# A hybrid block on one core: one channel tile of the depthwise convolution on GpSimd, the mLSTM's row normalisation on ScalarE

## The chip, the cores and the metric

The kernel runs on one NeuronCore of a Trainium2 chip. The metric is the device time of one launch in microseconds (us). A profile of one execution goes with it; in it PE is TensorE, PEld its weight loads, DVE is VectorE, ACT is ScalarE, POOL is GpSimd and SP is SyncE, which here issues the DMAs. "L494" is line 494 of the kernel before.

## The reference, cut to what matters

Two layers (`l = 0, 1`) over a sequence of 512 tokens and a context of 256, width 1024. Each layer has a token mixer with three branches and a squared-ReLU MLP. All is float32.

```python
def conformer_conv(a, w_dw, b_dw, g, b, w_pw):
    val, gate = jnp.split(a, 2, axis=-1)
    h = val * jax.nn.sigmoid(gate)
    h = lax.conv_general_dilated(h, w_dw[:, None, :], (1,), ((15, 15),),      # 31 taps, each of
                                 feature_group_count=CONV_DIM) + b_dw          # 512 channels alone
    return jax.nn.silu(layer_norm(h, g, b)) @ w_pw

def mlstm_out(h, o_pre, g, w):                  # h: mLSTM forward + backward, 4 heads of 128
    mu = jnp.mean(h, -1, keepdims=True)
    var = jnp.mean(jnp.square(h - mu), -1, keepdims=True)
    h = ((h - mu) * lax.rsqrt(var + LN_EPS)).reshape(bsz, t, ML_DIM) * g
    return (jax.nn.sigmoid(o_pre) * h) @ w

def token_mixer(...):
    a, qkv, o_pre, g_if, cq, ckv, kr, gates = jnp.split(u @ w_in + b_in, IN_SPLITS, axis=-1)
    y_conv = conformer_conv(a, ...)
    y_ml = mlstm_out(mlstm_bidir(...), ...)     # chunks of 128 tokens, state carried from chunk to chunk
    o_x = mla_blockwise(...)                    # latent attention, 8 heads
    return gated_merge(gates, y_conv, y_ml, o_x @ w_mla_out, w_out, b_out)
```

In layer 0 sequence and context (768 columns) go through all of it; in layer 1 the convolution, the gates and the MLP see the 512 sequence columns alone.

## The kernel before, in words

**Layout.** Activations lie channel-major: 128 channels on the partitions, up to 768 tokens along the free axis. The layer's input `u` is eight such tiles. The convolution's 512 channels are four tiles, `hc[0]` to `hc[3]`, with an accumulator `ca[j]` each.

**Products.** Every large product is made of three passes over a high and a low part of both operands (`mm3`, L266 to L268). A weight tile comes by DMA (`wr`), ScalarE makes its high part `wh` (L261), and the low part `wl` is a subtraction `wr - wh` (L262). That subtraction is on VectorE, except for the weights of the 24 gate tiles and the four output-gate tiles, where `plan()` names GpSimd. Weights are fetched two ahead (`LOOK = 2`); raw, high and low part have three buffers each.

**The stage around the change**, in each layer, in the order of the program:

1. Four times value and gate of the convolution: two products, ScalarE's identity and tanh, and one VectorE instruction (L511) make `hc[j]`.
2. V, gates of the mLSTM and the key's rotary part (L526 to L548): 2 x 6 groups of 24 products, each evacuated from one of the two `pg` tiles of PSUM by VectorE (L541, L544, L548).
3. Cumulated gates, scans and exponentials on 36 rows (L551 to L615), then the K and Q products (L618 and L640).
4. The mLSTM: six chunks in each direction (`mstep`). When both directions of a row tile are there, `mnorm` normalises it: `bn_stats` and `bn_aggr` per head on VectorE, `EPS` added (L745), the power -0.5 on GpSimd (L746), and per head one VectorE instruction, subtract the mean and multiply by the power (L748).
5. The 24 gate products, each with a tanh and a store to DRAM. After the eleventh the convolution's layer norm is done (`ln_fm`, L784), which reads all four `ca`.

**The taps.** `conv_taps()` is a generator. For each of four channel tiles it issues one VectorE instruction for the middle tap with the bias (L488), and then for each of 30 other taps one fused multiply-add per segment (L494): `ca += hc[shifted] * w`. Layer 0 has two segments (512 and 256 columns, less the shift), layer 1 one. `some_taps(k)` draws k taps from the generator; calls stand between the steps of stages 1 to 5 (9 after each `hc[j]`, 2 in each group of stage 2, 4 and 5 after each K and Q product, 3 after each gate), and the rest is drawn before the layer norm. The modulation vectors for later (`mod_pieces`, L165) are drawn in the same way with `pull`.

**What sets the order.** Only the first products are put in order by hand. Elsewhere the program's order gives priorities and a planner lays each engine's instructions in one fixed queue; an instruction that waits holds all behind it on its engine. Tiles come from pools of fixed size: `slot()` takes one of the 35 buffers of the pool `gen`.

Of the kernel before, what the change touches and what calls it, by code (L numbers as in the profile page):

```python
# [44 lines left out]
def build(tc, I, out):  # L45
    nc = tc.nc
# [1 line left out]
    ctx = ExitStack()  # L48
    cp = ctx.enter_context(tc.tile_pool(name="const", bufs=1))
    wp = ctx.enter_context(tc.tile_pool(name="w", bufs=3))  # L50
    gp = ctx.enter_context(tc.tile_pool(name="gen", bufs=35))
    vp = ctx.enter_context(tc.tile_pool(name="v", bufs=12))
    mp = ctx.enter_context(tc.tile_pool(name="mw", bufs=8))
    sp = ctx.enter_context(tc.tile_pool(name="small", bufs=6))
# [398 lines left out]
    for l in range(L):  # L453
# [26 lines left out]
            return [(0, n, win(i, n)[:, :n])]  # L480

        def conv_taps():
            for j in range(4):
                acc = slot("ca")
                ca.append(acc)
                wd = lambda t: col(l, "w_dw", j * CK + t)
                h = hc[j]
                V.tensor_scalar(acc[:, :n], h[:, :n], wd(15), col(l, "b_dw", j), op0=OP.mult, op1=OP.add)  # L488
                for d in [x for i in range(1, 16) for x in (-i, i)]:
                    for s0, s1 in ((0, S), (S, n)):  # L490
                        if s1 <= s0:
                            continue
                        a, b = max(s0, s0 - d), min(s1, s1 - d)
                        V.scalar_tensor_tensor(acc[:, a:b], h[:, a + d:b + d], wd(15 + d), acc[:, a:b],  # L494
                                               op0=OP.mult, op1=OP.add)
                    yield

        taps = None

        def some_taps(k):  # L500
            for _ in range(k):
                next(taps, None)

        for j in range(4):
            val, tg = slot("val"), slot("tg")
            for c0, c1, ps in conv_in(MT_VAL + j):
                A.activation(val[:, c0:c1], ps, AF.Identity, bias=HB(MT_VAL + j), scale=0.5)
            for c0, c1, ps in conv_in(MT_GATE + j):
                A.activation(tg[:, c0:c1], ps, AF.Tanh, bias=HB(MT_GATE + j), scale=0.5)
            h = slot("hc")  # L510
            V.scalar_tensor_tensor(h[:, :n], tg[:, :n], 1.0, val[:, :n], op0=OP.add, op1=OP.mult)  # L511
            hc.append(h)
            if j == 0:
                taps = conv_taps()
            some_taps(9)


        vt = []
# [7 lines left out]
        for hf, w_n in ((0, VG0), (1, VG1)):  # L526
            ws = [wget("w_vg", l, hf * 2 + q) for q in range(2)]
            for tt in range(NT):
                ps = pg()
                t0 = tt * 128  # L530
                for k in range(8):
                    wh, wl = ws[k // 4]
                    a, b = (k % 4) * w_n, (k % 4 + 1) * w_n
                    uh, ul = u[k]
                    o = ps[:, :w_n]
                    PE.matmul(o, uh[:, t0:t0 + 128], wh[:, a:b], start=(k == 0), stop=False)  # L536
                    PE.matmul(o, uh[:, t0:t0 + 128], wl[:, a:b], start=False, stop=False)  # L537
                    mark[0] = PE.matmul(o, ul[:, t0:t0 + 128], wh[:, a:b], start=False, stop=(k == 7))  # L538
                some_taps(2)
                bo = hf * VG0  # L540
                V.tensor_tensor(vt[tt][:, 2 * hf:2 * hf + 2, 0:128], ps[:, 0:256].rearrange("p (h d) -> p h d", h=2),  # L541
                                bvg[:, bo:bo + 256].rearrange("p (h d) -> p h d", h=2), op=OP.add)
                if hf == 0:
                    V.tensor_tensor(gt[:, tt, :].rearrange("p (g j) -> p g j", g=4)[:, :, 0:4],  # L544
                                    ps[:, 256:272].rearrange("p (g j) -> p g j", g=4),
                                    bvg[:, 256:272].rearrange("p (g j) -> p g j", g=4), op=OP.add)
                else:
                    V.tensor_tensor(kr[:, tt, :], ps[:, 256:288], bvg[:, VG0 + 256:VG0 + 288], op=OP.add)  # L548
# [69 lines left out]
        for h in range(MH):  # L618
            ps = win(MT_K + h, T)
            t = slot("kT")  # L620
            A.activation(t, ps, AF.Identity, bias=kb[l][:, h:h + 1], scale=KSCALE)
            kT.append(t)
            some_taps(4)
        kinds = {}
        for name, src in (("g", g_), ("A", A_), ("W", W_), ("E", E_)):
            ps = pt()
# [13 lines left out]
        for h in range(MH):  # L640
# [1 line left out]
            t = slot("qT")  # L642
            A.activation(t[:, :n], ps[:, :n], AF.Identity, bias=B(MT_Q + h))
            qT.append(t)
            some_taps(5)


        cst_ = [cp.tile([128, 4, 129], F32, name=f"cs{l}{d}", tag=f"cs{d}") for d in range(2)]
# [88 lines left out]
        def mnorm(tt):  # L737
# [6 lines left out]
            rs = small(4, "mrs", 3)  # L744
            V.tensor_scalar(rs, mv.rearrange("p (h s) -> p h s", s=2)[:, :, 1], EPS, None, op0=OP.add)  # L745
            G.tensor_tensor(rs, rs, mhalf, op=OP.pow)  # L746
            for h in range(MH):
                V.tensor_scalar(hv[:, h, 0:128], hv[:, h, 0:128], mv[:, 2 * h:2 * h + 1], rs[:, h:h + 1],  # L748
                                op0=OP.subtract, op1=OP.mult)
            hnorm[tt] = hv  # L750

        for j in range(NT):
# [23 lines left out]
        for b in range(3):  # L776
            for mt in range(8):
                g = gate(b, mt)
                nc.sync.dma_start(z_dram[b, mt, :, :n], g[:, :n])
                some_taps(3)  # L780
                pull(2)
                if b * 8 + mt == 10:
                    some_taps(200)
                    ln_fm(ca, 4, groups, conv_emit)  # L784


# [507 lines left out]
```

## Time and profile before

| | |
|---|---|
| median of 3 runs | 2558.47 us (2554.23 to 2559.24) |
| the profiled execution's own time | 2557.35 us |
| its span in the profile | 2555.5 us |
| PE busy | 2470.4 us (97%) |
| DVE busy | 1580.6 us (62%) |
| ACT busy | 939.5 us (37%) |
| POOL busy | 298.7 us (12%) |
| taps (L494), both layers | 227.8 us in 360 instructions |
| normalisation on DVE (L748) | 19.4 us in 40 instructions |
| gate weights' low parts on POOL (L262) | 145.7 us in 56 instructions |
| granted PE clock | 0.993 |

Busy time is the time in which an engine has an instruction running; an engine that is blocked inside an instruction counts as busy. A line of a view by groups has line, engine, operation, output and inputs, shapes and count, then busy time, mean ns of one, and the engine's idle time just before them with what ended it. A timeline row has start, duration, engine, line, operation, operands and count. In a table by stretches each row has the length, and then the busy time of each engine with its number of instructions.

### The profile page before, as it was taken

What the parts mean: (1) busy time and instruction counts of PE and PEld (TensorE: products, weight loads), DVE (VectorE), ACT (ScalarE), POOL (GpSimd) and SP (SyncE); (2) the same over time, 40 slices, a digit from 0 to 9 for tenths busy, and PEclk for the clock granted to TensorE, in tenths of its full rate; (3) what the DMA queues carried; (4) which work ended last, traced back from release to release, by engine and by line L of the source; (5) the groups of instructions that cost most, each with busy time, mean ns of one, the idle gap of its engine ahead of it and who ended that gap; (6) DMA issues with size and microseconds to landing.
All of it is one profiled execution on the core that took longest, in us unless ns stands there. A gap on an engine that the chain in (4) does not pass through costs nothing.

```text
span 2555.5 us, 38339 instructions
## 1 busy us (share of the span) xinstructions
PE 2470.4 (97%) x15272; PEld 2163.8 (85%) x15272; DVE 1580.6 (62%) x2847; ACT 939.5 (37%) x1607; POOL 298.7 (12%) x235
## 2 busy tenths in 40 slices
PE   7899989999999999999999999999999999999997
PEld 5888878888888899888888888977888888888887
DVE  4999976363356777655554379996043567554456
ACT  3123323222457563222222253333324575432323
POOL 0002132203000021000000031023411001100002
PEclk9999999999999999999999999999999999999999
DMA  7122344466110654343342252233563106333333
GB/s 264 53 75 70 98 163 161 166 195 210 62 34 1 188 168 142 122 131 115 108 129 88 65 149 78 59 106 101 175 203 111 50 18 213 101 99 92 99 94 113
DMA packets 137235, 298.45 MB, mean 117 GB/s; under 512 B 13776, under 2 KB 55248, under 8 KB 137056
## 3 DMA queue, kind: packets, MB, share of 16 engines
q1 hardware_dynamic: 137056, 296.00, 36.9%
q8 instruction: 120, 1.97, 0.3%
q14 instruction: 59, 0.48, 0.1%
HBM read 265.49 MB, written 30.46 MB: 116 GB/s over the span
## 4 chain that ended last, share of the span: by engine, by line
PE 81%; DVE 9%; DMA 4%; ACT 2%; issue 2%; POOL 1%; SPq 0%; DVEq 0%; ACTq 0%; POOLq 0%
PE pg L266 21%; PE pg L267 21%; PE pg L268 21%; PE pt L1003 2%; PE pt L982 2%; PE pt L266 2%; PE pt L267 2%; PE pt L268 2%; DVE ca L494 2%; DMA wm<-w_mod 1%; DMA ml<-z_dram 1%; PE pg L536 1%; PE pg L538 1%; PE pg L537 1%; DVE st L315 1%
## 5 line engine op out<-in xcount | busy, mean ns | idle before, releaser
L261 ACT CAST wh<-wr 128x1024 fp32r<-128x1024 f32 (+1 forms) x328 | 345.6, 1055 | 1202.4 <-PE pg L267 825.5
L262 DVE TENSOR_TENSOR wl<-wr,wh 128x1024 fp32r<-128x1024 f32 (+2 forms) x272 | 338.6, 1246 | 410.1 <-ACT wh L261 406.3
L268 PE MATMUL pg<-uh,wl 128*128 128x512 f32 (+1 forms) x1280 | 456.3, 356 | 2.2 <-DVE wl L262 2.2
L266 PE MATMUL pg<-uh,wh 128*128 128x512 f32 (+1 forms) x1280 | 457.2, 357 | 1.2 <-ACT gt__17278 L760 1.2
L267 PE MATMUL pg<-ul,wh 128*128 128x512 f32 (+1 forms) x1280 | 455.5, 356 | 0.7 <-POOL ul L1171 0.6
L266 PE MATMUL pg<-hidh,wh 128*128 128x512 f32 (+1 forms) x832 | 285.4, 344 | 3.9 <-DVE mv L318 2.0
L267 PE MATMUL pg<-hidl,wh 128*128 128x512 f32 (+1 forms) x832 | 284.9, 342 | 0.0
L268 PE MATMUL pg<-hidh,wl 128*128 128x512 f32 (+1 forms) x832 | 284.2, 342 | 0.0
L266 PEld LDWEIGHTS pg<-uh,wh 128*128 128x128 f32 x1280 | 244.2, 191 | 35.4 <-issue 2.5
L268 PEld LDWEIGHTS pg<-uh,wl 128*128 128x128 f32 x1280 | 243.9, 191 | 34.4 <-DVE wl L262 2.7
L267 PEld LDWEIGHTS pg<-ul,wh 128*128 128x128 f32 x1280 | 244.1, 191 | 33.2 <-POOL ul L1171 1.0
L494 DVE SCALAR_TENSOR_TENSOR ca<-hc,cols,ca 128x511 f32<-128x511 f32 (+9 forms) x360 | 227.8, 673 | 2.4
L262 POOL TENSOR_TENSOR wl<-wr,wh 128x1024 fp32r<-128x1024 f32 x56 | 145.7, 2602 | 562.6 <-ACT wh L261 562.6
L267 PE MATMUL pg<-u2l,wh 128*128 128x512 f32 (+1 forms) x608 | 210.3, 347 | 0.3 <-POOL u2l L1082 0.2
L1139 DVE SCALAR_TENSOR_TENSOR acc<-pg,mod,acc 128x512 f32<-128x512 f32 (+1 forms) x168 | 106.0, 659 | 168.6 <-PE pg L268 168.6
L268 PE MATMUL pg<-u2h,wl 128*128 128x512 f32 (+1 forms) x608 | 210.1, 347 | 0.0
L266 PE MATMUL pg<-u2h,wh 128*128 128x512 f32 (+1 forms) x608 | 209.9, 347 | 0.0
L165 DVE SCALAR_TENSOR_TENSOR mda<-wm,sil,mda 128x512 f32<-128x512 f32 x224 | 176.2, 808 | 7.6 <-DMA wm<-w_mod 5.0
L266 PEld LDWEIGHTS pg<-hidh,wh 128*128 128x128 f32 x832 | 157.3, 190 | 25.3 <-issue 3.5
L321 POOL TENSOR_TENSOR rs<-rs,mhalf 128x1 f32<-128x1 f32 x30 | 24.4, 819 | 1298.5 <-DVE rs L320 1298.5
L267 PEld LDWEIGHTS pg<-hidl,wh 128*128 128x128 f32 x832 | 157.9, 190 | 18.7 <-DVE hidl L1129 1.6
L268 PEld LDWEIGHTS pg<-hidh,wl 128*128 128x128 f32 x832 | 157.7, 189 | 18.0
(359 smaller groups left out, 4754.1 us busy)
## 6 DMA issues: line engine op xcount, KB each, us to landing
wr<-w SPq DMA_DIRECT2D x140, 512.0 KB, 3.6
wr<-w_in_fm SPq DMA_DIRECT2D x104, 512.0 KB, 3.8
wm<-w_mod SPq DMA_DIRECT2D x192, 256.0 KB, 4.5
wr<-w_out SPq DMA_DIRECT2D x40, 512.0 KB, 3.9
ml<-z_dram SPq DMA_DIRECT2D x104, 128.0 KB, 2.8
ml<-z_dram SPq DMA_DIRECT2D x48, 256.0 KB, 4.4
z_dram<-ml SPq DMA_DIRECT2D x32, 256.0 KB, 4.5
dm<-m_dram SPq DMA_DIRECT2D x20, 256.0 KB, 4.4
```

What stands on the lines that cost most here:

```text
L165: ins = V.scalar_tensor_tensor(av[v], w, sil[:, k, v:v + 1], av[v], op0=OP.mult, op1=OP.add)
L261: A.copy(h[:, :n], r[:, :n])
L262: eng.tensor_sub(lo[:, :n], r[:, :n], h[:, :n])
L266: PE.matmul(ps, hs, xh, start=first, stop=False)
L267: PE.matmul(ps, hs, xl, start=False, stop=False)
L268: return PE.matmul(ps, ls, xh, start=False, stop=last)
L315: V.bn_stats(st[:, hf * 6:(hf + 1) * 6], ps)
L494: V.scalar_tensor_tensor(acc[:, a:b], h[:, a + d:b + d], wd(15 + d), acc[:, a:b], op0=OP.mult, op1=OP.add)
L536: PE.matmul(o, uh[:, t0:t0 + 128], wh[:, a:b], start=(k == 0), stop=False)
L982: PE.transpose(p2[:, y * 128:(y + 1) * 128], P[:, (k4 + y) * 128:(k4 + y + 1) * 128], ident)
L1003: PE.matmul(po[64 * i:64 * i + 64, :256], va[B_.k0 + k][:, h * 64:h * 64 + 64], B_.pts[i][k // 2][:, k % 2, :], start=(k == 0), stop=(k == ...
L1139: V.scalar_tensor_tensor(acc[mt][:, c0:c1], ps[:, c0:c1], mc[:, 40 + mt, v:v + 1], acc[mt][:, c0:c1], op0=OP.mult, op1=OP.add)
```

## The change

- `conv_taps()` now serves channel tiles 0 to 2. Tile 3 has a generator of its own, `pool_taps()`, on GpSimd. It has no fused multiply-add there: each tap is a multiplication of all columns into a scratch tile `pt` and one addition per segment onto `ca[3]`.
- `some_pool_taps(k)` draws from it: one in every third group of stage 2, 2 after each K product, Q product and gate, the rest ahead of the layer norm. VectorE's draws become 7, 1 or 2, 3, 3 and 2.
- The four accumulators are taken at the first tile instead of one by one.
- In `mnorm` a new VectorE instruction makes `-mean * power` for the four heads, and the four per-head instructions go to ScalarE as an activation with scale and bias.
- The pool `gen` has 38 buffers, and the program's scratch for DMA descriptors is set to 1024.

```diff
-    gp = ctx.enter_context(tc.tile_pool(name="gen", bufs=35))
+    gp = ctx.enter_context(tc.tile_pool(name="gen", bufs=38))
...
         def conv_taps():
-            for j in range(4):
-                acc = slot("ca")
-                ca.append(acc)
+            for j in range(3):
+                acc = ca[j]
...
-        taps = None
+        def pool_taps():
+
+            acc, h = ca[3], hc[3]
+            wd = lambda t: col(l, "w_dw", 3 * CK + t)
+            G.tensor_scalar(acc[:, :n], h[:, :n], wd(15), col(l, "b_dw", 3), op0=OP.mult, op1=OP.add)
+            for d in [x for i in range(1, 16) for x in (-i, i)]:
+                t = slot("pt")
+                G.tensor_scalar(t[:, :n], h[:, :n], wd(15 + d), None, op0=OP.mult)
+                for s0, s1 in ((0, S), (S, n)):
+                    if s1 <= s0:
+                        continue
+                    a, b = max(s0, s0 - d), min(s1, s1 - d)
+                    G.tensor_tensor(acc[:, a:b], acc[:, a:b], t[:, a + d:b + d], op=OP.add)
+                yield
+
+        taps = ptaps = None
...
+        def some_pool_taps(k):
+            for _ in range(k):
+                next(ptaps, None)
...
             if j == 0:
+                ca.extend(slot("ca") for _ in range(4))
                 taps = conv_taps()
-            some_taps(9)
+            some_taps(7)
+        ptaps = pool_taps()
...
-                some_taps(2)
+                some_taps(2 if hf else 1)
+                if tt % 3 == 2:
+                    some_pool_taps(1)
...
-            some_taps(4)
+            some_taps(3)
+            some_pool_taps(2)
...
-            some_taps(5)
+            some_taps(3)
+            some_pool_taps(2)
...
+            nm = small(4, "mnm", 3)
+            V.scalar_tensor_tensor(nm, mv.rearrange("p (h s) -> p h s", s=2)[:, :, 0], -1.0, rs,
+                                   op0=OP.mult, op1=OP.mult)
             for h in range(MH):
-                V.tensor_scalar(hv[:, h, 0:128], hv[:, h, 0:128], mv[:, 2 * h:2 * h + 1], rs[:, h:h + 1],
-                                op0=OP.subtract, op1=OP.mult)
+                A.activation(hv[:, h, 0:128], hv[:, h, 0:128], AF.Identity, bias=nm[:, h:h + 1], scale=rs[:, h:h + 1])
...
-                some_taps(3)
+                some_taps(2)
+                some_pool_taps(2)
                 pull(2)
                 if b * 8 + mt == 10:
                     some_taps(200)
+                    some_pool_taps(200)
                     ln_fm(ca, 4, groups, conv_emit)
...
-    nc = bacc.Bacc("TRN2", target_bir_lowering=False, num_devices=1)
+    nc = bacc.Bacc("TRN2", target_bir_lowering=False, num_devices=1, dynamic_dma_scratch_size=1024)
```

## The prediction

> **What bounds the kernel now.** I read the page first (span, engine totals, the digits over 40 slices), then the table of busy time by stretches, the waits of TensorE, and last the timelines of GpSimd and VectorE side by side.
>
> ```profile
> span 2555.5 us, 38339 instructions
> ...
> PE 2470.4 (97%) x15272; PEld 2163.8 (85%) x15272; DVE 1580.6 (62%) x2847; ACT 939.5 (37%) x1607; POOL 298.7 (12%) x235
> ...
> DVE  4999976363356777655554379996043567554456
> ```
>
> Over the whole span TensorE (PE) is the bound: 85.1 us of idle is all that any change to the other engines could win. But the digits show two places, one per layer, where VectorE (DVE) is full too. They are the convolution and the mLSTM, where this change acts. The table by stretches gives their size:
>
> ```profile
> core 0: us, PE busy (x) PEld busy (x) DVE busy (x) ACT busy (x) POOL busy (x), PEclk, DMA share, GB/s
> 100.00:150.00 50.00, 43.14 (x308) 42.20 (x307) 47.44 (x117) 8.94 (x11) 0.00 (x0) 0.93 0.17 49
> 150.00:200.00 50.00, 47.78 (x281) 41.77 (x280) 49.31 (x89) 14.69 (x24) 0.00 (x0) 0.97 0.24 75
> 200.00:250.00 50.00, 48.30 (x318) 43.06 (x317) 48.43 (x106) 14.59 (x32) 15.07 (x5) 1.00 0.25 72
> 250.00:300.00 50.00, 44.79 (x311) 40.86 (x310) 47.11 (x116) 21.98 (x62) 8.66 (x4) 0.97 0.29 88
> 300.00:350.00 50.00, 41.80 (x252) 35.60 (x251) 44.93 (x112) 10.07 (x17) 14.03 (x8) 0.93 0.47 147
> 1575.00:1625.00 50.00, 50.00 (x357) 48.22 (x356) 44.98 (x104) 12.76 (x15) 0.00 (x0) 1.00 0.19 59
> 1625.00:1675.00 50.00, 46.68 (x260) 39.96 (x258) 48.77 (x63) 15.16 (x25) 7.28 (x3) 1.00 0.27 78
> 1675.00:1725.00 50.00, 47.70 (x295) 42.16 (x296) 47.45 (x96) 20.58 (x56) 9.51 (x4) 0.97 0.35 102
> ```
>
> In layer 0 DVE is busy for 237.2 of 250 us; in layer 1 for 141.2 of 150. PE idles 24.2 and 5.6 us there. The waits of PE, from 100 to 420 us (four rows) and from 1570 to 1800 us (the last), say for whom:
>
> ```profile
> PE pt L173 <- DVE mda L165: 9.7, 2, 8.0
> PE pg L536 <- DVE gt L544: 6.9, 1, 6.9
> ...
> PE pt L694 <- DVE dm L672: 2.8, 2, 2.6
> PE pg L268 <- DVE wl L262: 2.2, 1, 2.2
> ...
> PE pt L725 <- DVE kw L719: 4.2, 2, 4.0
> ```
>
> Together 25.8 us, always for something late in DVE's queue. That is about all that a lighter DVE can win. A heavier DVE has no such limit, since it has hardly 5% left to give.
>
> **What GpSimd costs DVE.** GpSimd (POOL) is idle for the 165 us before 203.48 us (the last fence has that row), so its work looks free. It isn't: the timeline shows what happens when both read SBUF (each row as its engine's timeline gives it; the last row is the tap of the convolution with minimum/median/maximum in ns).
>
> ```profile
> 211.81 2.82 POOL L262 TENSOR_TENSOR wl<-wr,wh 128x1024 fp32r<-128x1024 f32 x1 [2.75 <-ACT wh L261]
> 212.29 2.62 DVE L494 SCALAR_TENSOR_TENSOR ca<-hc,cols,ca 128x254 f32<-128x254 f32 x1
> ...
> 220.20 3.28 POOL L262 TENSOR_TENSOR wl<-wr,wh 128x1024 fp32r<-128x1024 f32 x1 [5.57 <-ACT wh L261]
> 221.50 1.28 DVE L672 TENSOR_TENSOR dm<-dm,pt 128x512 f32<-128x512 f32 x2 [0.28 <-PE pt L670]
> ...
> 1542.49 3.79 POOL L1171 TENSOR_TENSOR ul<-uf,uh 128x256 fp32r<-128x256 f32 x3
> 1543.59 1.23 DVE L511 SCALAR_TENSOR_TENSOR hc<-tg,val 128x512 f32<-128x512 f32 x1
> ...
> 347.48 4.72 DVE L165 SCALAR_TENSOR_TENSOR mda<-wm,sil,mda 128x512 f32<-128x512 f32 x7
> 347.89 7.36 POOL L262 TENSOR_TENSOR wl<-wr,wh 128x1024 fp32r<-128x1024 f32 x1 [16.91 <-ACT wh L261]
> ...
> L494 DVE SCALAR_TENSOR_TENSOR ca<-hc,cols,ca x360: 457/731/2898, 57.2 to 1720.6; 128x511 f32<-128x511 f32 x12, 128x510 f32<-128x510 f32 x12, 128x509 f32<-128x509 f32 x12, 128x508 f32<-128x508 f32 x12
> ```
>
> The 254-column tap began 0.48 us behind the POOL subtraction and ended 0.28 us after it: 2.62 us where the shortest of all taps takes 0.46 and the median one, of some 500 columns, 0.73. L672, with one input in PSUM, ran under another POOL subtraction undisturbed, 1.28 us for two. From 1542 us three short POOL instructions take 3.79 us instead of 3 x 0.73 (price below), and L511, as wide as a wide tap, 1.23 us: they take turns. So a tap on DVE and a POOL instruction that reads SBUF exclude each other.
>
> The Trainium skill states this as a rule (SBUF — State Buffer, section "Who interferes with whom"): a DVE instruction with two SBUF inputs, and a GpSimd one that reads SBUF, hold a shared port for a whole instruction each, and the one that starts first blocks the other. The trace agrees, with 2.62 us at 212.29 and the turns at 1542.49. The page speaks against any tap on GpSimd while taps run on DVE.
>
> **The change part by part.** The rows for the prices: taps by layer; L748, L745 and L746 with minimum/median/maximum; POOL's instructions where DVE left them alone.
>
> ```profile
> 50.00:350.00 300.00, 132.26 (x240) 0.97 0.28 85
> 1540.00:1725.00 185.00, 95.56 (x120) 0.99 0.28 84
> ...
> L748 DVE TENSOR_SCALAR hacc<-hacc,mmv,mrs x40: 334/343/2412, 246.3 to 1757.1; 128x128 f32<-128x128 f32 x40
> L745 DVE TENSOR_SCALAR mrs<-mmv x10: 153/160/170, 245.0 to 1752.9; 128x4 f32<-128x4 f32 x10
> ...
> L262 POOL TENSOR_TENSOR wl<-wr,wh 128x1024 fp32r<-128x1024 f32 x12 | 28.6, 2386 | 39.4 <-ACT wh L261 39.4
> L806 POOL TENSOR_TENSOR ml<-ml 128x512 f32<-128x512 f32 x16 | 20.6, 1288 | 131.0 <-DMA z_dram<-ml 68.3 <-DMA wr<-w_in_fm 38.2 <-DVE ml L803 15.6
> L1082 POOL TENSOR_TENSOR u2l<-uf,u2h 128x256 fp32r<-128x256 f32 x5 | 3.5, 731 | 0.0
> L887 POOL COPY kraw<-kr 128x256 f32<-128x256 f32 x6 | 2.1, 400 | 42.1 <-PE pg L267 42.1
> ```
>
> *Removed from DVE.* A quarter of the taps: 33.1 us in layer 0, 23.9 in layer 1 (the mean pair of a wide and a narrow tap in layer 0 is 1.10 us). L748: 24 and 16 instructions of 0.343 us, 8.2 and 5.5 us. Against it one new 4-column instruction per row tile, as L745: 10 x 0.16, 1.0 and 0.6 us. The first instruction of the tile's accumulator is under 1 us a layer and left out. Net relief: 40.3 and 28.8 us.
>
> *Added to POOL.* Per tap a multiplication into a scratch tile and an addition per segment. Two-input additions follow the rows: 0.731 us for 256 columns, 1.288 for 512, 2.386 for 1024, so 2.14 ns a column; 503 columns cost 1.27 us, 248 cost 0.71. No POOL multiplication by a column appears in this trace. Its nearest row is the copy, also with one tensor input, 0.400 us for 256. Taking half the two-input slope beyond that gives 0.95 us for 768 columns and 0.67 for 512. The upper bound is the two-input price, 1.84 and 1.29. I take the copy's, as the operand count is the same. Layer 0: 0.95 + 30 x (0.95 + 1.27 + 0.71) = 89 us (upper 116); layer 1: 0.67 + 30 x (0.67 + 1.27) = 59 (upper 78).
>
> For the multiplication the Trainium skill (GPSIMD Engine Reference, section 4.1) has one-input instructions roughly at line rate; at its 1.2 GHz that would be an estimate of 0.64 us of streaming for 768 columns, and some 8 us less in layer 0 by that price. No run here shows it.
>
> *What of POOL's time DVE pays.* Only while DVE has nothing but two-SBUF-input work. After the change, of DVE's remaining 124 us between 100 and 250 us, taps and L262 alone are 61%:
>
> ```profile
> 100.00:250.00 150.00, 83.90 (x151) 0.97 0.22 65
> ...
> 100.00:250.00 150.00, 12.43 (x10) 14.05 (x4) 0.97 0.22 65
> ```
>
> (83.90 x 0.75 + 12.43 over 145.2 - 21.0.) Scans, masks and row updates with two SBUF inputs come on top; I take 75%, and 70% in layer 1, where more PSUM reads lie between. Bounds: all of it (everything collides), none (POOL runs only under PSUM reads and in DVE's idle time). Blocked: 0.75 x 89 = 67 us and 0.70 x 59 = 41 us.
>
> *Sum on DVE.* +67 - 40.3 = +27 in layer 0, +41 - 28.8 = +12 in layer 1. The stretches have 12.8 and 8.8 us of DVE idle; half of that is usable, since the other half lies behind waits for data: 6.4 and 4.4. So DVE's end of work moves by +20 and +8 us. DVE feeds PE directly (weights' low parts, V's evacuation through two PSUM tiles, the mLSTM's products), so I pass that on in full: +28 us. By the bounds of price and share it runs from -25.8 (no blocking, every DVE wait of PE gone) to 116 + 78 - 69 - 11 = +114.
>
> *At nothing.* The 40 normalisations on ScalarE: 40 of some 0.39 us, as the mLSTM's exponentials have it, 16 us on an engine busy for 9 to 22 of 50 us. They are first read by the transposes of L816:
>
> ```profile
> L666 ACT ACTIVATE dm<-dm,colg 128x128 f32<-128x128 f32 x80 | 24.6, 393 | 10.7 <-DVE dm L664 10.7
> ...
> L816 PE MATMUL pt<-cst,hacc x40: 271/273/273, 530.1 to 1789.7; 128*128 128x128 f32 x40
> ```
>
> 530.1 us is nearly 200 us behind the last normalisation of layer 0; without that cover they would cost 16 us. DVE still waits for the power on POOL as today, now at the new 4-column instruction, with the mLSTM's next steps queued behind it. Three more slots and the four accumulators taken at once cost no instruction. The smaller descriptor scratch touches no transfer: the page's queues are hardware ones, issued by SP. No DMA moves.
>
> On the profiled execution's own 2557.35 us (1.1 below the median of 2558.47): 2557 + 28 = **2585 us**.
>
> **The rivals.**
>
> *DVE keeps the port (faster).* From 347.48 seven DVE instructions ran back to back without delay, while the POOL subtraction waited: 7.36 us instead of 2.39. If dense tap runs hold the port like this, POOL creeps through PSUM reads and DVE's idle time and blocks little. Then about 85% of the 25.8 us of DVE waits goes: 2557 - 22 = 2535 us. For it: those two rows. Against it: 211.81 and 1542.49, where POOL got in after one DVE instruction. The skill's rule that the first to start wins leaves both open.
>
> *POOL's own queue becomes the bound (slower still).* 91 chain instructions in layer 0, from the last convolution input at about 102.6 us, each of 0.98 us and behind one DVE instruction of some 0.6, end at 246 us. The first weight subtraction of the gates on POOL comes today at 203.48 us. Queued behind the chain it is up to 42 us late, and PE waits at the gates; the powers of the normalisation stand in the same queue. With layer 1 as in my case (8 us) that gives 2607 us if it swallows DVE's delay of 20 us and 2627 if it comes on top; I take 2617. It decides once the planner puts the chain ahead of those subtractions. Against it: the program asks for only 20 of 30 taps before the gates, and PE arrives there late anyway.
>
> ```profile
> 203.48 5.59 POOL L262 TENSOR_TENSOR wl<-wr,wh 128x1024 fp32r<-128x1024 f32 x1 [165.25 <-ACT wh L261]
> 101.68 0.95 DVE L511 SCALAR_TENSOR_TENSOR hc<-tg,val 128x768 f32<-128x768 f32 x1
> ```
>
> *A wash.* With 50% of POOL's time blocked, 44 and 30 us stand against 40 and 29: within noise of 2557.
>
> That the change doesn't do what it says I exclude: the engine is written out in each call.
>
> **How the numbers follow.** My case has 52% (2565 to 2615), the kept port 25%, POOL's queue 13%, the wash 10%. A difference under 0.2% (5 us) can't be told from none. So faster 0.25, same 0.10, slower 0.65. The range 2535 to 2640 leaves out about half of the faster case and the worst of the queue case.
>
> **What would show it.** Right: tap instructions on DVE with means well above 0.73 and 0.46 us, POOL's additions above 1.27 and 0.71, DVE still near full from 100 to 350 us, and PE waits for DVE (V's evacuation, low parts) above 25.8 us. Wrong: taps at their old means and PE waits near zero (the kept port); PE waiting for POOL at the gates (the queue); or a multiplication on POOL far from 0.95 us. If PE doesn't wait although DVE is blocked, passing the delay on in full was the error.

## The result and the profile after

The changed kernel takes **2617.74 us** (median of 4 runs, 2615.17 to 2618.67) against 2557.44 us before (median of 4): 1.0231 times as long, 95% interval 1.0218 to 1.0244. The forecast was 2585 us in a range of 2535 to 2640. The sign was right; the loss of 60 us is twice the 28 forecast.

The page of the changed kernel, its span, totals and digits of VectorE:

```profile
span 2616.7 us, 38400 instructions
...
PE 2481.2 (95%) x15272; PEld 2169.1 (83%) x15272; DVE 1586.1 (61%) x2725; ACT 954.5 (36%) x1647; POOL 544.8 (21%) x387
...
DVE  4996877454346676765555479895234567644456
```

The span grew by 61.2 us. PE's idle time is 135.5 us instead of 85.1, which is 50.4 of it. The other 10.8 us are PE's busy time (2470.4 before), with the same count of matmuls. In the stretch from 250 us, in which PE's longest wait ends, the granted clock is 0.81 in the table below, where before it was 0.97. How much of the 10.8 us that makes isn't shown. VectorE's busy time, which the forecast let grow by 39 us, grew by 5.5.

Busy time by stretches after the change, columns as in the table before:

```profile
100.00:150.00 50.00, 40.84 (x287) 39.76 (x286) 47.87 (x71) 4.17 (x4) 45.56 (x28) 0.93 0.10 32
150.00:200.00 50.00, 45.24 (x260) 39.48 (x259) 49.37 (x84) 20.73 (x36) 34.65 (x22) 0.93 0.23 70
200.00:250.00 50.00, 40.66 (x250) 36.06 (x248) 38.65 (x68) 7.40 (x8) 37.12 (x13) 0.99 0.15 43
250.00:300.00 50.00, 33.43 (x215) 30.03 (x216) 35.20 (x83) 17.01 (x46) 30.30 (x21) 0.81 0.25 70
...
1625.00:1675.00 50.00, 41.71 (x277) 38.79 (x278) 47.82 (x85) 12.02 (x13) 42.43 (x27) 1.00 0.14 43
1675.00:1725.00 50.00, 45.11 (x250) 38.38 (x248) 36.88 (x43) 14.81 (x25) 17.07 (x10) 1.00 0.25 73
1725.00:1775.00 50.00, 40.02 (x245) 34.42 (x245) 47.12 (x78) 16.52 (x45) 34.19 (x20) 0.93 0.32 97
```

GpSimd is busy for 45.56 of the 50 us from 100 on. VectorE is as full there as before (47.87), but got through 71 instructions instead of 117. Behind 200 us it is no longer full: 38.65 and 35.20 of 50, although PE is at its worst there. That doesn't fit a kernel in which VectorE simply has more to do.

PE's longest waits in layer 0 (100 to 465 us) and, in the last row, layer 1 (1570 to 1870 us), each with the sum, the number of times and the longest in us:

```profile
PE pt L718 <- DVE dm L696: 22.6, 5, 20.3
PE pt L173 <- DVE mda L165: 12.1, 2, 10.5
...
PE pt L749 <- DVE kw L743: 9.9, 2, 8.6
```

And the groups of the taps and of the chain, as I call the fourth tile's instructions on GpSimd (busy us, mean ns, idle time before them); the first row is the taps' in the kernel before:

```profile
L494 DVE SCALAR_TENSOR_TENSOR ca<-hc,cols,ca 128x511 f32<-128x511 f32 (+9 forms) x360 | 227.8, 673 | 2.4
...
L493 DVE SCALAR_TENSOR_TENSOR ca<-hc,cols,ca 128x511 f32<-128x511 f32 (+11 forms) x270 | 201.1, 792 | 2.2
...
L504 POOL TENSOR_SCALAR pt<-hc,cols 128x768 f32<-128x768 f32 (+1 forms) x60 | 128.4, 2148 | 22.4 <-DMA m_dram<-ab 15.3 <-DVE kr L893 5.5 <-PE pt L577 1.6
L509 POOL TENSOR_TENSOR ca<-ca,pt 128x511 f32<-128x511 f32 (+14 forms) x90 | 108.3, 1223 | 0.7
```

The multiplication (L504) takes 2.15 us in the mean, over twice my 0.95 and 0.67. The taps left on VectorE have a mean of 792 ns where they had 673.

**How the longest wait comes about.** SP's timeline, then GpSimd's, then VectorE's, around PE's wait of 20.3 us. It ends at 264 us, behind the row transfer `dm<-m_dram`, which brings rows of the mLSTM's decay matrix. The third row of the first fence is the same transfer in the kernel before:

```profile
196.03 58.65 SPq L258 DMA_DIRECT2D wr<-w_in_fm  x6
254.77 0.94 SPq L686 DMA_DIRECT2D dm<-m_dram  x2
...
223.88 0.97 SPq L662 DMA_DIRECT2D dm<-m_dram  x2
```

```profile
213.03 20.12 POOL L262 TENSOR_TENSOR wl<-wr,wh 128x1024 fp32r<-128x1024 f32 x1 [12.88 <-ACT wh L261]
233.14 4.38 POOL L504 TENSOR_SCALAR pt<-hc,cols 128x768 f32<-128x768 f32 x2
237.49 3.71 POOL L509 TENSOR_TENSOR ca<-ca,pt 128x503 f32<-128x503 f32 x4
241.17 2.84 POOL L262 TENSOR_TENSOR wl<-wr,wh 128x1024 fp32r<-128x1024 f32 x1
243.99 4.81 POOL L504 TENSOR_SCALAR pt<-hc,cols 128x768 f32<-128x768 f32 x2
248.78 3.25 POOL L509 TENSOR_TENSOR ca<-ca,pt 128x502 f32<-128x502 f32 x4
252.00 2.33 POOL L262 TENSOR_TENSOR wl<-wr,wh 128x1024 fp32r<-128x1024 f32 x1
```

```profile
205.79 25.17 DVE L493 SCALAR_TENSOR_TENSOR ca<-hc,cols,ca 128x511 f32<-128x511 f32 x48
...
258.99 1.28 DVE L688 TENSOR_TENSOR dm<-dm,cst 128x512 f32<-128x512 f32 x1 [14.10 <-DMA dm<-m_dram]
```

VectorE runs 48 taps back to back at their old speed, and GpSimd's weight subtraction, begun at 213.03, gets nowhere until they end: 20.12 us instead of 2.39. The next two subtractions stand behind two rounds of the chain (two multiplications and four additions each) of 8 us. Each subtraction frees a weight buffer (`wr`) for which SP's queue waits. SP is held until the third one ends at 254.33 us, and the row transfer behind it leaves at 254.77 instead of 223.88 as before. Of these 31 us, 17 were lost earlier: the row transfer ahead of it left at 184.67 instead of 167.91. VectorE waits 14.10 us for the rows, and PE waits behind VectorE.

### The profile page after: what moved, and what is told of

Read it like the earlier page. It is cut to its first block, busy times and chain, and to the rows that moved or that the text cites. A ratio compares the mean times of both kernels' runs of the same rounds, so it can differ in the third digit from the quotient of the medians.

```text
span 2616.7 us, 38400 instructions
## 1 busy us (share of the span) xinstructions
PE 2481.2 (95%) x15272; PEld 2169.1 (83%) x15272; DVE 1586.1 (61%) x2725; ACT 954.5 (36%) x1647; POOL 544.8 (21%) x387
## 5 line engine op out<-in xcount | busy, mean ns | idle before, releaser
L262 POOL TENSOR_TENSOR wl<-wr,wh 128x1024 fp32r<-128x1024 f32 x56 | 156.2, 2790 | 274.0 <-ACT wh L261 263.2
L493 DVE SCALAR_TENSOR_TENSOR ca<-hc,cols,ca 128x511 f32<-128x511 f32 (+11 forms) x270 | 201.1, 792 | 2.2
L165 DVE SCALAR_TENSOR_TENSOR mda<-wm,sil,mda 128x512 f32<-128x512 f32 x224 | 182.9, 838 | 8.7 <-DMA wm<-w_mod 5.9
```

Of the source, the lines that this page charges most:

```text
L165: ins = V.scalar_tensor_tensor(av[v], w, sil[:, k, v:v + 1], av[v], op0=OP.mult, op1=OP.add)
L262: eng.tensor_sub(lo[:, :n], r[:, :n], h[:, :n])
```

## The experiments

Times are medians; a ratio stands against the kernel before, run beside it on the same chip, whose medians were 2557 to 2560 us. Diffs are against the changed kernel unless said otherwise.

### What the chain costs and what its absence is worth

**No chain.** GpSimd keeps only the fourth tile's middle tap; its 30 other taps are left out.

```diff
             for d in [x for i in range(1, 16) for x in (-i, i)]:
-                t = slot("pt")
-                G.tensor_scalar(...)
-                ... G.tensor_tensor(acc, acc, t)
                 yield
```

> The changed kernel, but GpSimd does only the middle tap of channel tile 3; its 30 other taps are left out, so that quarter of the convolution isn't computed. It shows what the relief of VectorE is worth alone. Port theory (a GpSimd instruction that reads SBUF excludes VectorE's two-SBUF-input instructions, and dense taps keep GpSimd's weight subtractions waiting) and queue theory (the chain delays what stands behind it in GpSimd's own queue): 2535 to 2550 us. Order theory (the new draws, the early slots or the ScalarE normalisation cost the time): still above 2595 us.

2554.79 us, 0.9982 (0.9973 to 0.9992). So the chain costs 63 us, and the whole relief of VectorE is worth 4. That is 5 us above the range of the port and queue theories, which counted on more from the relief. The page of this run and its taps:

```profile
PE 2475.2 (97%) x15272; PEld 2167.9 (85%) x15272; DVE 1519.8 (60%) x2725; ACT 954.5 (37%) x1647; POOL 311.4 (12%) x237
...
L493 DVE SCALAR_TENSOR_TENSOR ca<-hc,cols,ca 128x511 f32<-128x511 f32 (+11 forms) x270 | 170.1, 676 | 2.2
```

VectorE is busy for 61 us less than before, and PE has next to nothing of it.

**The chain on VectorE.** The same draws and slots, the fourth tile's taps as fused instructions on VectorE.

```diff
-                t = slot("pt")
-                G.tensor_scalar(...); G.tensor_tensor(...)
+                V.scalar_tensor_tensor(acc[:, a:b], h[:, a + d:b + d], wd(15 + d), acc[:, a:b], op0=OP.mult, op1=OP.add)
```

> The changed kernel with the same draws, slots and ScalarE normalisation, but tile 3's own chain is made of VectorE's fused multiply-adds. Port and queue theory: VectorE has its old work less some 12 us of normalisation, 2545 to 2565 us. Order theory: above 2595 us.

2558.11 us, 0.9994 (0.9985 to 1.0004). The new order of the draws is no cause. With the run ahead of it: 57 us of taps more or less on VectorE (226.7 against 170.1) move the time by 3 us.

**The normalisations alone**, on the kernel before.

```diff
+            V.scalar_tensor_tensor(nm, mv[..., 0], -1.0, rs, op0=OP.mult, op1=OP.mult)
             for h in range(MH):
-                V.tensor_scalar(hv[:, h, 0:128], ..., op0=OP.subtract, op1=OP.mult)
+                A.activation(hv[:, h, 0:128], ..., AF.Identity, bias=nm[:, h:h + 1], scale=rs[:, h:h + 1])
```

> The kernel before with the second part of the change alone: the mLSTM's rows normalised by ScalarE. My prediction: VectorE is relieved by 12 us in the stretches where TensorE waits for it, nothing new is late, 2548 to 2558 us. If the added step through ScalarE is a new wait, above 2562 us.

2554.10 us, 0.9985 (0.9976 to 0.9995): a gain of 4 us. That is as much as the run without chain has in all, so the taps' own relief isn't seen.

### Which of GpSimd's instructions cost the time

**The multiplication with two scalars**, the form of the chain's first instruction.

```diff
-                G.tensor_scalar(t[:, :n], h[:, :n], wd(15 + d), None, op0=OP.mult)
+                G.tensor_scalar(t[:, :n], h[:, :n], wd(15 + d), 0.0, op0=OP.mult, op1=OP.add)
```

> The changed kernel with GpSimd's multiplication written with two scalars (times the tap, plus 0.0), the form of the chain's first instruction, which took 0.98 us for 768 columns where the one-scalar form took 2.2 us undisturbed. If the price hangs on the form: about 1.2 us less for each of 30 in layer 0 and 0.7 us in layer 1, 36 and 20 us of GpSimd's time, of which three quarters and 70% blocked VectorE, so 27 and 14 us less: 2575 to 2595 us. If the price stays near 2.2 us: 2610 to 2622 us, and the first instruction's 0.98 us has another reason.

2617.78 us, 1.0230 (1.0215 to 1.0246). The groups of this run:

```profile
L493 DVE SCALAR_TENSOR_TENSOR ca<-hc,cols,ca 128x511 f32<-128x511 f32 (+11 forms) x270 | 205.8, 808 | 2.2
...
L504 POOL TENSOR_SCALAR pt<-hc,cols 128x768 f32<-128x768 f32 (+1 forms) x60 | 67.8, 1139 | 46.9 <-DMA m_dram<-ab 21.0 <-PE pt L577 16.0 <-DVE kr L893 9.8
```

The price did hang on the form: 60.6 us less on GpSimd. The time stayed, and so did the taps. What I expected, that VectorE pays by GpSimd's busy time, fell.

For the two runs that follow I set each VectorE instruction of the changed kernel's two stages (to 450 us, and 1500 to 1900 us) against the median of its like in the run without chain, and ascribed what it had over that to the GpSimd instruction that it overlapped most. That gives 47 us under the 90 additions and 20 us under the 60 multiplications.

**Multiplications alone**, the additions left out:

```diff
-                    G.tensor_tensor(acc[:, a:b], acc[:, a:b], t[:, a + d:b + d], op=OP.add)
```

> The changed kernel with GpSimd's 60 multiplications as they are and its 90 additions left out (the fourth tile then keeps only its middle tap). In the trace of the changed kernel VectorE's instructions ran over their usual length by 47 us under the additions and by 20 under the multiplications, though the multiplications lasted longer (128 against 108 us). Theory A (only a short part of a multiplication holds VectorE up): 2555 to 2572 us, close to the 2555 of the kernel without chain. Theory L (each GpSimd instruction costs by its length): 128 of 237 us of the chain are left, so more than half of the 63 us: 2585 to 2600 us.

**Additions alone**, the multiplications left out:

```diff
-                G.tensor_scalar(t[:, :n], h[:, :n], wd(15 + d), None, op0=OP.mult)
-                    G.tensor_tensor(acc[:, a:b], acc[:, a:b], t[:, a + d:b + d], op=OP.add)
+                    G.tensor_tensor(acc[:, a:b], acc[:, a:b], h[:, a + d:b + d], op=OP.add)
```

> The changed kernel with GpSimd's 90 additions as they are, reading the convolution's input in place of the scaled scratch tile, and its 60 multiplications left out (the taps' weights are then missing from the fourth tile). Theory A (the additions hold VectorE up): 2595 to 2618 us, nearly the whole loss. Theory L (by length): 108 of 237 us are left, 2575 to 2590 us.

2576.92 us, 1.0075 (1.0058 to 1.0092), and 2607.20 us, 1.0199 (1.0183 to 1.0214). The page and the tap group of the first, then of the second:

```profile
PE 2478.1 (96%) x15272; PEld 2169.4 (84%) x15272; DVE 1538.6 (60%) x2725; ACT 954.8 (37%) x1647; POOL 441.8 (17%) x297
...
L493 DVE SCALAR_TENSOR_TENSOR ca<-hc,cols,ca 128x511 f32<-128x511 f32 (+11 forms) x270 | 178.2, 704 | 2.2
```

```profile
PE 2486.2 (95%) x15272; PEld 2175.3 (83%) x15272; DVE 1577.6 (61%) x2725; ACT 955.1 (37%) x1647; POOL 433.1 (17%) x327
...
L493 DVE SCALAR_TENSOR_TENSOR ca<-hc,cols,ca 128x511 f32<-128x511 f32 (+11 forms) x270 | 215.8, 841 | 2.2
```

Against the run without chain, 130.4 us of multiplications made the same 2725 VectorE instructions 18.8 us longer and the kernel 22 us; 121.7 us of additions made them 57.8 us longer and the kernel 52. The whole chain: 66.3 and 63. So in this kernel, on average, a two-input addition holds VectorE up for about half of its time, a multiplication for about a seventh, and each microsecond of holding up is paid about in full. The multiplications cost 5 us more than theory A allowed. GpSimd's and VectorE's timelines of the first run show eight multiplications in a row, and five taps under them that keep their old speed:

```profile
107.69 22.47 POOL L504 TENSOR_SCALAR pt<-hc,cols 128x768 f32<-128x768 f32 x8
...
115.39 3.13 DVE L493 SCALAR_TENSOR_TENSOR ca<-hc,cols,ca 128x252 f32<-128x252 f32 x5
```

**Fills in place of the chain**: five fills of the scratch tile for each of the 30 taps, which read nothing (the fourth tile's taps are left out).

```diff
-                G.tensor_scalar(...); G.tensor_tensor(...)
+                for _ in range(5):
+                    G.memset(t[:, :n], 0.0)
```

> The changed kernel, but each of the 30 taps on GpSimd is replaced by five fills of the scratch tile with zeros, which write SBUF and read nothing; by the row of the one 768-column fill (0.74 us) they take 3.7 us a tap in layer 0, nearly what the multiplication and two additions take undisturbed (2.19 + 1.07 + 0.61). The taps of tile 3 are left out. Port theory: VectorE isn't blocked, taps at their old 0.73 and 0.46 us, 2540 to 2560 us. Queue theory: GpSimd is as busy as in the changed kernel, its weight subtractions come as late, 2600 to 2620 us. Order theory: above 2595 us.

2595.45 us, 1.0143 (1.0128 to 1.0158), between the two theories. VectorE's and GpSimd's timelines and PE's longest wait of this run show why:

```profile
103.20 35.85 DVE L487 TENSOR_SCALAR ca<-hc,cols 128x768 f32<-128x768 f32 x1
...
103.90 34.74 POOL L505 MEMSET pt<- 128x768 f32 x51
```

```profile
PE pg L552 <- DVE gt L562: 32.9, 1, 32.9
```

One middle tap of 0.9 us stood for 35.85 us while GpSimd did 51 fills in a row, and PE waited 32.9 us behind it. So I repeated it with the other tiles' middle taps on ScalarE:

```diff
-                V.tensor_scalar(acc[:, :n], h[:, :n], wd(15), col(l, "b_dw", j), op0=OP.mult, op1=OP.add)
+                A.activation(acc[:, :n], h[:, :n], AF.Identity, bias=col(l, "b_dw", j), scale=wd(15))
```

> The run with fills in place of the chain (five fills of the scratch tile for each of the 30 taps, some 175 us of GpSimd's time, reading nothing; the fourth tile keeps only its middle tap), with the middle taps of the other three tiles on ScalarE, where the run before had one VectorE instruction standing for 35.9 us. Theory R (it is GpSimd's reads that hold VectorE's two-input instructions up): the taps keep their old length and the time is near that of the kernel without chain, 2552 to 2566 us. Rival (any busy GpSimd costs, by its writes or its queue): 2585 to 2605 us.

2562.64 us, 1.0013 (1.0004 to 1.0023). Its groups of fills and taps:

```profile
L505 POOL MEMSET pt<- 128x768 f32 (+1 forms) x300 | 174.0, 634 | 28.7 <-DMA m_dram<-ab 21.8 <-DVE ropey L887 4.1 <-DVE ca L493 2.7
...
L493 DVE SCALAR_TENSOR_TENSOR ca<-hc,cols,ca 128x511 f32<-128x511 f32 (+11 forms) x270 | 171.5, 683 | 4.6 <-ACT ca L487 2.5
```

174 us of fills cost the taps 1.4 us (170.1 us without chain). The kernel is 8 us slower than without chain. So what holds the taps up is GpSimd's reads; its writes alone held up the middle tap, an instruction with one tensor input, and cost little where that was out of the way.

### Where the time is paid

**The row transfer from ScalarE's queue** instead of SP's.

```diff
-                nc.sync.dma_start(dv, m_dram[l, d, None, :, c0:c1].to_broadcast([128, 4, 128]))
+                nc.scalar.dma_start(dv, m_dram[l, d, None, :, c0:c1].to_broadcast([128, 4, 128]))
```

> The changed kernel with one edit: the row transfer of the decay matrix (dm<-m_dram) is issued from ScalarE's queue instead of SP's. Theory S (the starved weight subtraction of GpSimd holds SP's queue, and with it this transfer): TensorE's wait of 20.3 us at L718 falls below 6 us and the time to 2590 to 2605 us. Theory P (VectorE loses its time at the port, and the late transfer only stands in for that): the wait moves to another instruction behind VectorE and the time stays at 2612 to 2622 us.

2603.63 us, 1.0178 (1.0161 to 1.0195). PE's waits in layer 0:

```profile
PE pt L173 <- DVE mda L165: 15.2, 2, 13.5
PE pt L718 <- DVE dm L696: 5.8, 4, 4.1
```

L718's 20.3 us are gone, and 14 us of the time; 3 of the gain go to the next wait. SP's queue is a place where the loss is paid, not the cause of all of it.

**Half of the chain**: the 14 inner taps of the fourth tile (|d| up to 7) fused on VectorE, 16 on GpSimd.

```diff
             for d in [x for i in range(1, 16) for x in (-i, i)]:
+                if abs(d) <= 7:
+                    ... V.scalar_tensor_tensor(acc[:, a:b], h[:, a + d:b + d], wd(15 + d), acc[:, a:b], ...)
+                    continue
                 t = slot("pt")
```

> The changed kernel with 14 of the 30 taps of the fourth tile (the inner ones) back on VectorE as fused instructions, 16 left on GpSimd. Theory P (the loss grows with GpSimd's busy time): 2617.7 less 14/30 of 60, so 2583 to 2597 us. Theory S (the loss is a few stalls that need a full queue): the stall at the gates goes altogether, and the time falls by more than its share, below 2575 us; or it stays whole, above 2605 us.

2595.00 us, 1.0138 (1.0123 to 1.0154), as theory P has it. VectorE's timeline and PE's longest wait in layer 0:

```profile
193.24 42.83 DVE L493 SCALAR_TENSOR_TENSOR ca<-hc,cols,ca 128x511 f32<-128x511 f32 x48
```

```profile
PE pt L727 <- DVE dm L705: 27.3, 3, 24.8
```

The same run of 48 taps that took 25.17 us in the changed kernel takes 42.83 here, because here GpSimd got its turns in between, and the product `dm` stands behind it on VectorE. In both runs, whichever engine wins the turns, PE waits over 20 us.

**The gates' low parts on VectorE**, first in the changed kernel, then as a control in the kernel before.

```diff
             for i in range(MT_G, MT_G + 24):
-                yield fm(i, G)
+                yield fm(i)
             for i in range(MT_O, MT_O + 4):
-                yield fm(i, G)
+                yield fm(i)
```

> The changed kernel with the low parts of the gates' weights on VectorE instead of GpSimd, as V's weights have them. Theory S (their starvation at 213 us, 20.1 us instead of 2.4, makes the largest stall): the stall of TensorE at L718 goes and the time falls to 2590 to 2605 us, in spite of some 1.2 us more of VectorE's time for each weight tile. Theory P: VectorE is only heavier, 2615 to 2632 us.

> The control of the run before: the kernel before, with the low parts of the gates' weights on VectorE and nothing else changed. Theory S (the 43 us that this edit won in the changed kernel come from the weight subtractions that stood between GpSimd's chain and SP's queue): without the chain nothing stands there, and the edit is worth nothing, 2553 to 2562 us, or costs a little. Rival (the edit is good by itself, whatever the chain): 2515 to 2545 us.

2574.93 us, 1.0059 (1.0044 to 1.0074), and 2529.46 us, 0.9892 (0.9877 to 0.9906). The first is below both expectations, the second the rival's. Without the control the first would have looked like proof that the starved subtraction makes most of the loss: 43 us less. But the edit wins 28 us without any chain, so my theory S accounts for 15 of the 60 us if the two effects simply add, and the chain still costs 45 where GpSimd has nothing else of weight to do. The page of the control:

```profile
PE 2468.3 (98%) x15272; PEld 2164.5 (86%) x15272; DVE 1592.2 (63%) x2903; ACT 939.1 (37%) x1607; POOL 156.9 (6%) x179
...
L262 DVE TENSOR_TENSOR wl<-wr,wh 128x1024 fp32r<-128x1024 f32 (+1 forms) x328 | 410.3, 1252 | 447.3 <-ACT wh L261 443.9
```

56 subtractions more, 70 us by the mean of 1.252, raised VectorE's busy time by only 11.6 us (from 1580.6), and PE's idle time fell to 58.7 us. The tuned kernel was itself paying for GpSimd's two-input instructions. Whether all of the gain comes from VectorE's shorter instructions, or part of it from weight buffers that come free sooner, this run doesn't separate.

**Two combinations with it**: the two-scalar multiplication, and that with the row transfer from ScalarE's queue.

> The changed kernel with the low parts of the gates' weights on VectorE and the multiplication with two scalars. Theory P (what is left of the loss, 15 us, is the time for which GpSimd's reads block VectorE): the chain is 57 us shorter, and with a third to a half of that on VectorE's path the time falls to 2545 to 2562 us. Theory N (VectorE pays one instruction's delay for each of GpSimd's instructions, whatever its length, or the loss lies elsewhere): 2568 to 2580 us, as when the multiplication alone was made shorter.

> As the run ahead of it, and the row transfer of the decay matrix from ScalarE's queue as well. With the weight subtractions gone from GpSimd, SP's queue still waits for VectorE's subtractions. Theory S (that transfer is late wherever SP waits for a weight buffer): another 5 to 12 us less than the run ahead of it. Theory P: no difference beyond 4 us.

2582.38 us, 1.0101 (1.0079 to 1.0122), and 2581.07 us, 1.0093 (1.0077 to 1.0108). The first is above both expectations. Shorter multiplications are worth nothing again, here even minus 7 us; why they cost something isn't shown. The 5 to 12 us expected of the row transfer are missing: without the subtractions on GpSimd no instruction waits for it any more, where VectorE waited 14.10 us in the changed kernel.

### When the chain runs

**Late draws**: the low parts on VectorE, and all taps of the chain drawn at the gates (three for each), none in the stages of V, K and Q; then the same with the two-scalar multiplication.

```diff
-                if tt % 3 == 2:
-                    some_pool_taps(1)
...
-            some_pool_taps(2)
...
-            some_pool_taps(2)
...
                 some_taps(2)
-                some_pool_taps(2)
+                some_pool_taps(3)
```

> The changed kernel with the low parts of the gates' weights on VectorE (2574.9 us so far), and with the chain's taps drawn only at the gates, three for each, none in the stages of V, K and Q. Theory F (the loss is blocking that bunches ahead of the gates, where the relief is small): K and Q end as early as without the chain, and the time falls to 2540 to 2562 us. Rival (the blocking only moves into the gates' stage, where VectorE also has the mLSTM): 2568 to 2590 us.

> The run with the chain drawn late (2585.0 us, in which TensorE waited 23.6 and 14.6 us at L314 for the chain's last addition), with the multiplication with two scalars, some 36 and 20 us shorter a layer. If the chain's own length is what those waits come from: they go, and the time falls by 30 to 38 us, to 2547 to 2556 us. If VectorE's turns, not the multiplications, set the pace of the chain: 2570 to 2586 us.

2584.98 us, 1.0106 (1.0091 to 1.0121), and 2556.10 us, 0.9990 (0.9980 to 1.0000). The first lies in the range of its rival, but for a cause that neither side named: PE waits for the chain's end, in layer 0 and in layer 1:

```profile
PE pt L314 <- POOL ca L509: 23.6, 1, 23.6
...
PE pt L314 <- POOL ca L509: 14.6, 1, 14.6
```

In the second the waits are 2.7 and 6.4 us. Here alone the multiplication's price decides: drawn late, the chain's own length is on the path, and 29 us go with it. The early draw had hidden the length and paid by blocking; drawn late and short, the chain costs 27 us over the control's 2529.46 instead of 53.

### The better kernel

**Low parts and normalisations**, without a chain: the two edits above on the kernel before.

> The kernel before with the low parts of the gates' weights on VectorE (2529.5 us alone) and ScalarE's normalisations (4 us alone), no chain on GpSimd. If the two gains add up: 2523 to 2528 us. If the normalisations won only what VectorE lost under GpSimd's subtractions: 2527 to 2533 us.

2527.74 us, 0.9881 (0.9864 to 0.9897). That is 2 us below the low parts alone, within the interval of either run, and in both expectations' ranges: whether the gains add up can't be told. The low parts make nearly all of it.

**Normalisations and the row transfer from ScalarE's queue**, on the kernel before.

> The kernel before with ScalarE's normalisations and the row transfer of the decay matrix from ScalarE's queue; no chain on GpSimd. Theory S (the transfer is late only because of the chain): as with the normalisations alone, 2551 to 2557 us. Rival (SP's queue costs the kernel before something too): 2540 to 2550 us.

2553.58 us, 0.9985 (0.9975 to 0.9994): as the normalisations alone. In the kernel before, no time hangs on that transfer.

## Why the prediction was right in sign and half in size

**The bound: right, but read too generously.** "About all that a lighter DVE can win" was 25.8 us. Without the chain 61 us of VectorE's busy time went, and 4 us of the time. The taps are filler, drawn between the instructions on which PE waits; a tap less mostly left VectorE idle.

**The exclusion: right for the additions, not for the multiplication.** The fills, which read nothing, left the taps at 171.5 us, the additions brought them to 215.8. The Trainium skill's rule (SBUF — State Buffer, section "Who interferes with whom"), that a two-input DVE instruction contends with GpSimd's reads and not with its writes alone, agrees with both numbers. But the prediction took every GpSimd instruction that reads to block for its whole length, as it read that rule. The multiplications read too, and 130.4 us of them left the taps at 178.2 us, against 170.1 without; there the measurement decides.

**GpSimd's prices: the additions near, the multiplication wrong.** The additions' mean of 1.22 us includes VectorE's turns; the shortest took 1.06 and 0.61, where the forecast pair was 1.27 and 0.71. The multiplication, priced by the copy at 0.95 and 0.67, took at least 2.20 us for 768 columns and 1.56 for 512, above even my upper bound. The term was mis-sized by 64 us (30 x 1.25 + 30 x 0.89), yet it is not why the loss was larger: with the two-scalar form the time stayed at 2617.78. (The 8 us that the prediction works out beside its 0.64 us are 9 by its own prices.)

**The share: too high.** I had 67 + 41 = 108 us of VectorE's time blocked, by GpSimd's length. The run pair without and with the chain gives 66.3, nearly half of the additions' time and a seventh of the multiplications'.

**The sum on DVE: this step failed.** It set blocked time off against relief, us for us ("+67 - 40.3 = +27"). By that rule, with the measured sizes, 66.3 us blocked against 60.8 relieved (1580.6 less 1519.8) would be a wash, and VectorE's busy time did end where it began (+5.5). But the two are not the same kind of time. Relief is taken from filler and is worth 4 us; blocking falls on whatever VectorE has next, and all that stands behind it, and costs 63. The difference, 59, is nearly the measured 60. My +28 came of two errors that partly cancel: blocking too large by 42 us, and relief and idle time counted at 69 + 11 instead of 4. That the sum had the right sign is in part luck.

**Passing on in full: right** for the blocking, in this order of the draws. Three sizes of it (18.8, 57.8 and 66.3 us) cost 22, 52 and 63. It is no law: drawn late and short, the chain cost only 27 us.

**The signs.** Longer taps and longer waits of PE for VectorE came as named. VectorE near full from 100 to 350 us did not: from 200 to 300 it was busy for 38.65 and 35.20 of 50 us. And a multiplication far from 0.95 us was named as a sign of being wrong.

**At nothing.** The normalisations were right, and better by 4 us. "No DMA moves" was true of the program and wrong of the queue: SP waits for buffers that GpSimd frees, so the row transfer left 31 us later (17 of them lost earlier), and its removal from SP's queue won 14 us.

**The rivals.** VectorE keeping the port was seen (20.12 us at 213.03), and it didn't make the kernel faster. GpSimd's queue ahead of the gates, for which I took 2617 us, has the measured number by luck: its mechanism carries about a quarter of the loss, 15 us by the control. A wash was what my own sum would have given with the true sizes.

**What stays open.** Why VectorE's blocked time wasn't taken up by the time that the relief had set free is shown in part only. In the changed kernel VectorE is full from 100 to 200 us (47.87 and 49.37 of 50) and idles behind, so the free time came too late there. The 20.12 us of starvation stood in the run without chain too, as GpSimd's timeline of that run has it, and the time was none the worse:

```profile
192.25 20.12 POOL L262 TENSOR_TENSOR wl<-wr,wh 128x1024 fp32r<-128x1024 f32 x1 [86.92 <-ACT wh L261]
```

That it hurts only with the chain's rounds behind it is argued from this, not shown alone. Which engine wins the turns isn't settled either. At 213.03 a GpSimd subtraction begun within a run of taps was kept out; in layer 1 one in the same position got in at once, as GpSimd's and VectorE's timelines of the changed kernel have it, and the 20 taps took 24.02 us:

```profile
1709.84 2.58 POOL L262 TENSOR_TENSOR wl<-wr,wh 128x1024 fp32r<-128x1024 f32 x1 [32.93 <-ACT wh L261]
```

```profile
1705.49 24.02 DVE L493 SCALAR_TENSOR_TENSOR ca<-hc,cols,ca 128x511 f32<-128x511 f32 x20
```

## What to carry to other kernels

Don't net work taken from an engine against time for which that engine is blocked: price the first by the waits that it ends, which may be none when it is filler, and the second, until a run shows less, in full. An idle GpSimd is not free while VectorE runs two-input work, and that holds for the GpSimd instructions that a tuned kernel has already: moving 56 subtractions back to VectorE won 28 us. An edit that mends a changed kernel has to be run on the kernel before as well, or its own gain is taken for proof of the cause.

## What the hardware showed that I had not expected

- GpSimd's multiplication of 768 columns by one per-partition scalar took at least 2.20 us; with a second scalar and an addition in the same instruction, 0.90. The Trainium skill (GPSIMD Engine Reference, section 4.1) has one-input instructions roughly at line rate; at the clock of 1.2 GHz that the page gives, that is an estimate of 0.64 us. The measured 2.20 differs, and the measurement decides. The longer form held VectorE up no longer than the short one.
- One VectorE instruction of 0.9 us, with one input and two scalars, stood for 35.85 us behind 51 fills of GpSimd in a row, and a GpSimd subtraction of 2.39 us for 20.12 us under 35 taps. In these two cases an instruction that lost its turn did not get the next one; in layer 1 a subtraction got in at once.
- PE's granted clock fell to 0.81 in the stretch with its longest stall, and its busy time rose by 10.8 us with no more work (by 4.8 in the run without chain).
